# RMS norm with each row written twice: the order of loads and stores on one DMA queue, and the first loads

## The chip, the core and the metric

The kernel runs on one core of a Trainium2 chip. The time is device microseconds of one execution; 12 runs of the kernel before lie between 240.41 and 242.0 us, with a median of 241.0. A profiled execution also leaves a trace, whose span runs from the first to the last instruction. Engines are named as in the profile: ACT is ScalarE, DVE is VectorE, POOL is GpSimd, SP is SyncE; a trailing q (SPq, ACTq) is that engine's instruction queue, where transfers are issued and semaphores waited for. The transfers run on the core's 16 DMA engines.

## The reference

```python
B, S, D = 8, 512, 2048            # float32
x_rep = np.repeat(x, 2, axis=1)   # every row twice: (8, 1024, 2048)
rms = np.sqrt((x_rep ** 2).mean(axis=-1, keepdims=True) + 1e-6)
return (x_rep / rms * gamma[None, None, :]).astype(np.float32)
```

x has 4096 rows of 8 KB (33.6 MB). Each row is divided by its root mean square, multiplied by gamma, and written twice (67.1 MB).

## The kernel before

The 4096 rows are cut into 8 tiles of 512. A tile lies in SBUF as 128 partitions with K = 4 consecutive rows of x in each, so a partition's share of a load is one contiguous run of 32 KB, and its share of a store one run of 64 KB, because the repeated rows are consecutive too. One buffer `y` holds both: eight row slots in each partition, of which a load fills the upper four, and the compute writes the results to all eight. A pool of three such buffers (L39) serves the eight tiles, so tile i + 3 is loaded into the buffer of tile i, once that has been stored.

`load(i)` (L45 to L53) issues the load of tile i on SP's queue, whole (4 MB) or in `parts`. `compute` (L82) goes through a tile's four rows per partition: ACT squares a row with a running sum (L64) and takes the root (L68); DVE takes the reciprocal (L73) and multiplies the row by it and by gamma in one instruction (L74); the second copy of the row (L80) is made by ACT, for the last row of a call by DVE. ACT's square of the next row is put ahead of its copy of this one. `store(i)` (L55) issues the store of 8 MB, also on SP's queue.

The order is written by hand (`manual_schedule`, L94), and on each engine instructions go in program order. SP first issues tile 0 in four quarters (L95), then tiles 1 and 2 (L101, L102). Then, for every tile, comes its store (L108), and from tile 1 on, the load of the tile two further (L109 to L110), which has to wait until the store of the tile one before has landed, because it reuses its buffer. So the queue holds load 0, 1, 2, store 0, 1, load 3, store 2, load 4, store 3, and so on to store 7; tile 7 is loaded and stored in halves. A wait of SP for a computed tile or for a free buffer holds up all that SP issues behind it.

Gamma (8 KB) is loaded by one DMA from ACT's queue to one partition (L97); POOL broadcasts it to all 128 (L98). Every DMA from SP or ACT signals one of eight completion semaphores, which are given out in turn in the order of the program. At the end of the program (L136) SP waits for the semaphores in turn, and then all engines meet.

Of the kernel before, what the change touches and what calls it, by code (L numbers as in the profile page):

```python
# [1 line left out]

# [4 lines left out]


@with_exitstack
def kernel(  # L10
    ctx: ExitStack,
    tc: tile.TileContext,
    x: bass.AP,
    gamma: bass.AP,
    out: bass.AP,
):
    nc = tc.nc
    P = nc.NUM_PARTITIONS
    f32 = mybir.dt.float32
    Act = mybir.ActivationFunctionType  # L20
    Alu = mybir.AluOpType

    B, S, D = x.shape
    Bo, So, Do = out.shape
    R = So // S
    assert R == 2 and D == Do and B == Bo and So == S * R
    eps = 1e-6
    inv_d = 1.0 / float(D)


    K = 4
    N = B * S
    assert N % (P * K) == 0
    ntiles = N // (P * K)
    x_t = x.rearrange("b s d -> (b s) d").rearrange("(n p k) d -> n p k d", p=P, k=K)
    out_t = out.rearrange("b s d -> (b s) d").rearrange("(n p j) d -> n p (j d)", p=P, j=K * R)

    singles = ctx.enter_context(tc.tile_pool(name="singles", bufs=1))
    rows = ctx.enter_context(tc.tile_pool(name="rows", bufs=3))  # L39
    junk = ctx.enter_context(tc.tile_pool(name="junk", bufs=1, space=bass.MemoryType.PSUM))  # L40
    small = ctx.enter_context(tc.tile_pool(name="small", bufs=8))

    ys = []

    def load(i, eng, parts=1):  # L45


        y = rows.tile([P, K * R, D], f32, name="y")
        step = K // parts
        for k in range(0, K, step):  # L50
            at = K * (R - 1) + k
            eng.dma_start(out=y[:, at : at + step, :], in_=x_t[i, :, k : k + step, :])  # L52
        ys.append(y)  # L53

    def store(i, k0, k1):  # L55
        nc.sync.dma_start(  # L56
            out=out_t[i, :, R * k0 * D : R * k1 * D],
            in_=ys[i][:, R * k0 : R * k1, :].rearrange("p j d -> p (j d)"),
        )

    def square(i, k):
        sq = junk.tile([P, D], f32, name="sq")
        ss = small.tile([P, 1], f32, name="ss")
        nc.scalar.activation(  # L64
            out=sq[:], in_=ys[i][:, K * (R - 1) + k, :], func=Act.Square, accum_out=ss[:]
        )
        rms = small.tile([P, 1], f32, name="rms")
        nc.scalar.activation(out=rms[:], in_=ss[:], func=Act.Sqrt, scale=inv_d, bias=eps_t[:])  # L68
        return rms

    def scale(i, k, rms):
        rstd = small.tile([P, 1], f32, name="rstd")
        nc.vector.reciprocal(out=rstd[:], in_=rms[:])  # L73
        nc.vector.scalar_tensor_tensor(  # L74
            out=ys[i][:, R * k, :], in0=ys[i][:, K * (R - 1) + k, :], scalar=rstd[:], in1=gamma_b[:],
            op0=Alu.mult, op1=Alu.mult,
        )

    def repeat(i, k, copy):
        copy(out=ys[i][:, R * k + 1, :], in_=ys[i][:, R * k, :])  # L80

    def compute(i, k0, k1):  # L82

        rms = square(i, k0)
        for k in range(k0, k1):
            scale(i, k, rms)
            if k + 1 < k1:
                rms = square(i, k + 1)
                repeat(i, k, nc.scalar.copy)
            else:  # L90
                repeat(i, k, nc.vector.tensor_copy)


    ctx.enter_context(tc.manual_schedule())  # L94
    load(0, nc.sync, parts=K)  # L95
    gamma_b = singles.tile([P, D], f32, name="gamma_b")
    nc.scalar.dma_start(out=gamma_b[0:1, :], in_=gamma.partition_broadcast(1))  # L97
    nc.gpsimd.partition_broadcast(out_ap=gamma_b[:], in_ap=gamma_b[0:1, :])  # L98
    eps_t = singles.tile([P, 1], f32, name="eps_t")
    nc.vector.memset(eps_t, eps)  # L100
    load(1, nc.sync)  # L101
    load(2, nc.sync)  # L102

    for i in range(ntiles):
        parts = 2 if i == ntiles - 1 else 1
        for k in range(0, K, K // parts):
            compute(i, k, k + K // parts)
            store(i, k, k + K // parts)  # L108
        if i >= 1 and i + 2 < ntiles:  # L109
            load(i + 2, nc.sync, parts=2 if i + 3 == ntiles else 1)  # L110


# [1 line left out]
_INS = ['x', 'gamma']  # L114
_OUTS = [((8, 1024, 2048), 'float32')]


# [23 lines left out]
```

## Time and profile before

| | |
|---|---|
| median of 12 runs | 241.0 us (240.41 to 242.0) |
| the profiled execution | 240.41 us, span 238.6 us |
| ACT busy | 115.6 us (48%) |
| DVE busy | 90.8 us (38%) |
| queue q1 (all of x and the output), share of 16 DMA engines | 98.5% |
| moved | 100.69 MB, 422 GB/s over the span |
| load of a whole tile, median from issue to landing | 34.2 us |

The share of a queue is the time that its packets took, over 16 engines times the span. The time from issue to landing holds the time in which a transfer stands in the queue behind earlier ones; it is no measure of a transfer's own length. Idle time of an engine that isn't the bottleneck costs nothing.

### The profile page before, as it was taken

The page shows a single profiled execution, that of the slowest core. Times are in us where ns is not written, and L with a number is a line of the kernel's source. Part 1 is how long each engine was busy: PE and PEld are TensorE (multiplying, and loading weights), DVE is VectorE, ACT ScalarE, POOL GpSimd, SP SyncE. Part 2 cuts the span into 40 slices and gives each one's busy share as a digit, 9 for nine tenths or more (in the row PEclk, how much of TensorE's full clock was granted, in tenths as well). Part 3 has the DMA queues.
Part 4 walks back from the last instruction along what each step waited for, and adds up shares of the span by engine and source line. Part 5 has one row for each costly group of instructions (what it writes and reads, how often), then busy time and mean ns, then how long its engine had stood idle before and what let it go on. Part 6 is the DMA issues. An engine that isn't in the chain of part 4 may idle for free.

```text
span 238.6 us, 298 instructions
## 1 busy us (share of the span) xinstructions
DVE 90.8 (38%) x74; ACT 115.6 (48%) x121; POOL 2.5 (1%) x5
## 2 busy tenths in 40 slices
DVE  0477749671000084500864007630167219900000
ACT  2998999970000299203990049900598059600000
POOL 4000000000000000000000000000000000000000
DMA  7999998989899999999898999989998899898995
GB/s 261 430 453 439 439 439 352 527 352 527 352 434 423 450 450 397 417 428 516 352 527 352 428 450 463 417 385 439 472 461 385 385 434 522 385 494 352 434 434 220
DMA packets 3028, 100.69 MB, mean 422 GB/s; under 512 B 337, under 2 KB 337, under 8 KB 337
## 3 DMA queue, kind: packets, MB, share of 16 engines
q1 hardware_dynamic: 3024, 100.66, 98.5%
q10 hardware_dynamic: 2, 0.01, 0.0%
q14 instruction: 2, 0.02, 0.0%
HBM read 33.56 MB, written 67.11 MB: 422 GB/s over the span
## 4 chain that ended last, share of the span: by engine, by line
DMA 66%; ACT 13%; DVE 7%; SPq 1%; issue 0%
DMA y<-in_x_dram 39%; DMA out_dram<-y 27%; ACT sq L64 7%; DVE y L74 6%; ACT y L80 5%; ACT rms L68 1%; DVE y L80 1%; SPq L52 1%; DVE rstd L73 0%; SPq L56 0%
## 5 line engine op out<-in xcount | busy, mean ns | idle before, releaser
L64 ACT ACTIVATE sq<-y 128x2048 f32<-128x2048 f32 x32 | 59.9, 1872 | 85.7 <-DMA y<-in_x_dram 85.7
L74 DVE SCALAR_TENSOR_TENSOR y<-y,rstd,gamma_b 128x2048 f32<-128x2048 f32 x32 | 75.3, 2352 | 1.2
L73 DVE RECIPROCAL rstd<-rms 128x1 f32<-128x1 f32 x32 | 5.2, 162 | 116.0 <-ACT rms L68 116.0
L80 ACT COPY y<-y 128x2048 f32<-128x2048 f32 x23 | 43.4, 1888 | 3.7 <-DVE y L74 3.7
L80 DVE COPY y<-y 128x2048 f32<-128x2048 f32 x9 | 11.0, 1227 | 0.3
L68 ACT ACTIVATE rms<-ss,eps_t 128x1 f32<-128x1 f32 x32 | 9.4, 294 | 1.0
L64 ACT ACTIVATION_READ_ACCUMULATOR sq<-y 128x1 f32 x32 | 6.0, 186 | 0.0
L98 POOL PARTITION_BROADCAST gamma_b<-gamma_b x1 | 2.3, 2295 | 2.3 <-DMA gamma_b<-in_gamma_dram 2.3
L64 ACT ACT_TABLE_LOAD x1 | 1.3, 1283 | 1.3 <-PEq L125 1.3
L68 ACT ACT_TABLE_LOAD x1 | 1.3, 1283 | 0.0
L100 DVE MEMSET eps_t<- 128x1 f32 x1 | 0.1, 59 | 0.8 <-PEq L125 0.8
L125 POOL MEMSET const-bfloat16-1.0<- 128x1 bf16 x1 | 0.1, 102 | 0.0
L125 POOL MEMSET const-uint8-127<- 128x1 uint8 x1 | 0.1, 102 | 0.0
L125 POOL MEMSET const-float32-0.0<- 128x1 f32 x1 | 0.1, 99 | 0.2 <-issue 0.2
L125 POOL MEMSET const-float32-1.0<- 128x1 f32 x1 | 0.1, 100 | 0.0
## 6 DMA issues: line engine op xcount, KB each, us to landing
y<-in_x_dram SPq DMA_DIRECT2D x6, 4096.0 KB, 34.2
out_dram<-y SPq DMA_DIRECT2D x2, 4096.0 KB, 27.1
y<-in_x_dram SPq DMA_DIRECT2D x4, 1024.0 KB, 7.8
y<-in_x_dram SPq DMA_DIRECT2D x2, 2048.0 KB, 36.4
out_dram<-y SPq DMA_DIRECT2D x7, 31.7
gamma_b<-in_gamma_dram ACTq DMA_DIRECT2D x1, 8.0 KB
```

Of the source, the lines that this page charges most:

```text
L52: eng.dma_start(out=y[:, at : at + step, :], in_=x_t[i, :, k : k + step, :])
L64: nc.scalar.activation(out=sq[:], in_=ys[i][:, K * (R - 1) + k, :], func=Act.Square, accum_out=ss[:])
L68: nc.scalar.activation(out=rms[:], in_=ss[:], func=Act.Sqrt, scale=inv_d, bias=eps_t[:])
L73: nc.vector.reciprocal(out=rstd[:], in_=rms[:])
L74: nc.vector.scalar_tensor_tensor(out=ys[i][:, R * k, :], in0=ys[i][:, K * (R - 1) + k, :], scalar=rstd[:], in1=gamma_b[:], op0=Alu.mult, o ...
L80: copy(out=ys[i][:, R * k + 1, :], in_=ys[i][:, R * k, :])
L98: nc.gpsimd.partition_broadcast(out_ap=gamma_b[:], in_ap=gamma_b[0:1, :])
L100: nc.vector.memset(eps_t, eps)
L125: nc = _bacc.Bacc("TRN2", target_bir_lowering=False, num_devices=1)
```

## The change

Three things change. Tile 0 is loaded in two halves instead of four quarters. Gamma is loaded by four DMAs of 2 KB instead of one of 8 KB; the number of DMAs ahead of the stores also shifts which of the eight semaphores each later DMA signals, the last store's among them. And the loads in the loop are issued in pairs: after the stores of tiles 0 and 1 come loads 3 and 4, after the stores of 2 and 3 loads 5 and 6, after those of 4 and 5 load 7, which is in halves as before. Each load still waits for the store that frees its buffer.

```diff
-    load(0, nc.sync, parts=K)
+    load(0, nc.sync, parts=2)
     gamma_b = singles.tile([P, D], f32, name="gamma_b")
-    nc.scalar.dma_start(out=gamma_b[0:1, :], in_=gamma.partition_broadcast(1))
+    for c in range(0, D, D // 4):
+        nc.scalar.dma_start(
+            out=gamma_b[0:1, c : c + D // 4], in_=gamma[c : c + D // 4].partition_broadcast(1)
+        )
     nc.gpsimd.partition_broadcast(out_ap=gamma_b[:], in_ap=gamma_b[0:1, :])
...
             store(i, k, k + K // parts)
-        if i >= 1 and i + 2 < ntiles:
-            load(i + 2, nc.sync, parts=2 if i + 3 == ntiles else 1)
+
+        if i % 2 == 1:
+            for j in (i + 2, i + 3):
+                if j < ntiles:
+                    load(j, nc.sync, parts=2 if j + 1 == ntiles else 1)
```

## The prediction

> **What bounds the kernel now.** I read the totals and the slices first, then the queues, then the times at which SP issues each transfer, and last the start and the end.
>
> ```profile
> span 238.6 us, 298 instructions
> DVE 90.8 (38%) x74; ACT 115.6 (48%) x121; POOL 2.5 (1%) x5
> ...
> DMA  7999998989899999999898999989998899898995
> ...
> q1 hardware_dynamic: 3024, 100.66, 98.5%
> ...
> HBM read 33.56 MB, written 67.11 MB: 422 GB/s over the span
> ```
>
> No engine is busy for half of the span, while queue q1, which carries every load of x and every store, keeps the 16 DMA engines at work for 98.5% of it. The kernel is a single stream of transfers in the order in which SP issues them. It can only become faster by moving the bytes at a better rate, by losing less where one transfer gives way to the next, or at the two ends.
>
> ```profile
> 0.72 3.31 SPq L52 DMA_DIRECT2D y<-in_x_dram  x6
> 23.85 16.16 SPq L56 DMA_DIRECT2D out_dram<-y  x2
> 52.72 0.34 SPq L52 DMA_DIRECT2D y<-in_x_dram  x1
> 54.45 0.33 SPq L56 DMA_DIRECT2D out_dram<-y  x1
> 72.27 0.34 SPq L52 DMA_DIRECT2D y<-in_x_dram  x1
> 98.86 0.33 SPq L56 DMA_DIRECT2D out_dram<-y  x1
> 101.56 0.34 SPq L52 DMA_DIRECT2D y<-in_x_dram  x1
> ```
>
> This is the timeline of SP. Call the loads L0 to L7 and the stores S0 to S7 (L7 and S7 have halves a, b). L3 goes out at 52.72, when S0 has landed, L4 at 72.27 (S1 landed), L5 at 101.56 (S2 landed). By the trace's semaphore events a whole load takes 9.4 to 9.9 us (L2, just ahead of the first store, 10.7) and a whole store 19.3 to 19.7 us, one behind the other, so the queue is never dry.
>
> ```profile
> SPq L56 <- DVE y L80: 156.4, 9, 26.5
> SPq L52 <- DMA out_dram<-y: 36.6, 5, 17.5
> SPq L136 <- DMA out_dram<-y: 28.1, 3, 9.6
> ```
>
> These are SP's own waits. They are long because SP runs ahead; they cost only if a transfer is issued after the engines have run out of earlier ones.
>
> The trace also records each packet (start, bytes, duration). Undisturbed packets are very regular: 8 KB 0.309 us, 16 KB 0.61, 32 KB 1.21, 64 KB 2.418, that is 26.5 to 27.1 GB/s on each of 16 engines. What the packets took above these, summed and divided by 16, is 2.3 us: 0.54 in the first 6 us; 1.05 at 27 to 34 us, where L2 gives way to S0; 0.06, 0.11, 0.10, 0.11 and 0.10 at the five later places where a load gives way to a store; at most 0.05 in each stretch between, so a store that gives way to a load costs about nothing, nor does load after load or store after store. In each place it is the last load packets that are stretched. The 16 engines also drift apart: the spread between the first and the last one's landing is 0.6 us at S0 and 1.6 us at S7b, the end at 237.66.
>
> **The change part by part.** The sum is made against the profiled execution: 240.41 us, a span of 238.6 and 1.8 around it. It is the fastest of the 12 runs, 0.59 under their median of 241.0, so I add 0.59 at the end.
>
> *Order of the queue.* Before: L0 L1 L2 S0 S1 L3 S2 L4 S3 L5 S4 L6 S5 L7 S6 S7, six turns from load to store. After: L0 L1 L2 S0 S1 L3 L4 S2 S3 L5 L6 S4 S5 L7 S6 S7, four. Two of the five small turns go: 0.48 us / 5 x 2 = 0.19 us. Drift grows by 1.6 - 0.6 = 1.0 us over those five turns, and about half of the spread lies beyond the mean engine; two turns fewer save 1.0 x 0.5 x 2/5 = 0.2 us at the last engine, an estimate.
>
> Does the queue stay full? With 9.7 us a load, 19.4 a store and 17.0 us from a tile's landing to its store (tile 3: first square at 81.84, store issued at 98.86), the new stream runs L3 to 81.8, L4 91.5, S2 110.9, S3 130.3, L5 140.0, L6 149.7, S4 169.1, S5 188.5, L7 198.2, S6 217.6. The new wait is L4's on S1: SP issues L4 at 72.2, with L3 (9.7 us) still ahead. Behind that wait stands S2, computed by about 57; it goes out at 72.6 and is needed at 91.5. S3 can go out at 81.8 + 17.0 = 98.8, needed at 110.9. L5 waits for S2 (110.9) with S3 ahead, L6 for S3 (130.3) with L5 ahead, S4 is behind L6 on SP (130.7, needed at 149.7), S5 goes at 157.0 (needed at 169.1), S6 near 173 (198.2), S7a near 202 (217.6). Every cover is 9 us or more, so these waits cost nothing.
>
> *Tile 0 in two halves.* Per engine 32 packets of 8 KB become 16 of 16 KB: 32 x 0.309 = 9.89 against 16 x 0.611 (median of L7's packets) = 9.78 us, so 0.11 us less. SP issues two transfers fewer, 0.45 us each, hidden behind packets in flight. But the first square waits for 2 MB:
>
> ```profile
> 5.49 1.88 ACT L64 ACTIVATE sq<-y 128x2048 f32<-128x2048 f32 x1 [2.95 <-DMA y<-in_x_dram]
> ...
> 22.55 1.23 DVE L80 COPY y<-y 128x2048 f32<-128x2048 f32 x1
> ```
> ```profile
> L56 SPq EVENT_SEMAPHORE  x13: 17/6262/16983, 7.9 to 202.8; - x13
> ```
>
> The first of SP's semaphore waits on L56 marks the landing of the second quarter, 7.9. So compute of tile 0 starts 2.4 us later, and S0 goes out at 23.85 + 2.4 = 26.3. Its packets are first needed when L2's last ones end, from 30.4 on: 4 us of cover instead of 6.5. Tiles 1 and 2 follow 2.4 us later too (S1 near 42, needed at 52.6). Cost 0.
>
> On the number of transfers the trace and the Trainium skill can be weighed. The four quarters of L0 land at 5.49, 7.94, 10.43 and 12.93 us, 2.49 us apart for 1.05 MB, which is 421 GB/s, so a queued transfer pays no fixed price. The skill's page "DMA: Bandwidth & Descriptors", section "Anatomy of one DMA — SWDGE (gpsimd) path", fits a DMA as 2.0 us plus its bytes at 436 GB/s; if these queued loads paid that, two fewer would save 4 us and the sum would be 236.4. I go by the row.
>
> *Gamma in four DMAs.* One 8 KB packet becomes four of 2 KB, each with its own issue on ACT's queue and its own semaphore, and POOL's broadcast waits for all four.
>
> ```profile
> 0.71 0.51 ACTq L97 DMA_DIRECT2D gamma_b<-in_gamma_dram  x1
> ...
> 1.26 1.28 ACT L64 ACT_TABLE_LOAD   x1 [1.26 <-PEq L125]
> 2.75 2.29 POOL L98 PARTITION_BROADCAST gamma_b<-gamma_b  x1 [2.33 <-DMA gamma_b<-in_gamma_dram]
> ```
>
> Four issues end near 0.71 + 4 x 0.54 = 2.9; from the end of an issue to the broadcast it was 2.75 - 1.22 = 1.5, so the broadcast runs from 4.4 to 6.7. ACT's table load ends near 4.2. The first use of gamma is at 9.40 before, so near 11.8 after: 5 us of cover; without it every us late would delay S0, which has 4 more to give. The packets share one engine with x: gamma's packet took 0.764 us; at best four cost what one did (0), at worst 4 x 0.764 - 0.764 = 2.3 us on that engine. I take 0, since no engine stands out in the landings of the first quarter (spread 0.44 us).
>
> A rule against small transfers stands in the same page's "Rules for kernel authors": coalesce, since under 64 KB one mostly pays overhead. Its 2 us in turn for each DMA would put the broadcast at 8.7 to 11.0, an estimate from that page that would still be hidden.
>
> *The end.* S7b's semaphore moves from the sixth to the seventh of eight, and SP's closing waits go through them in turn. Behind S7b's landing the trace has two more of these, 0.06 us apart (237.68, 237.74, 237.80); one is left: 0.06 us saved.
>
> Sum: 0.19 + 0.2 + 0.11 + 0.06 = 0.56 us, 240.41 - 0.56 = 239.85, and 0.59 added for the median: **240.4 us**.
>
> **The rivals.** 0.2% of 241.0 is 0.48 us, about what a measurement of this kernel can tell from no change.
>
> *A. The turn gets dearer behind two loads (slower).* L2 to S0 costs 1.05 us and follows 29 us without a store; the small turns cost 0.10 and follow 9.7 us. If the price grows with that stretch, a turn after two loads (19.4 us) costs 0.10 + 0.95 x 9.7 / 19.3 = 0.58 by a straight line. L4 to S2 and L6 to S4 are such turns, L7 to S6 stays: 2 x 0.58 + 0.10 = 1.26 against 0.48, so 0.78 lost, 0.17 saved by the other terms, 241.0 + 0.6 = 241.6; at the full 1.05 each, 242.5. It decides from 0.28 us a turn. Against it: L2 to S0 is also the first store of all, and each of the small turns is a tenth of it.
>
> *B. Nothing reaches the end.* The engine that ends last may not be the one that lost most at the two turns; then 0.06 to 0.17 us remain, 240.9.
>
> *C. Gamma's four packets hold one engine back.* At the worst price that engine ends 2.3 us later, from a mean end of 236.4 to 238.7 against the last engine's 237.33: 1.4 us lost, less the rest, near 242.0. It decides once that engine ends later than the others.
>
> **How the numbers follow.** Forecast 0.57, A 0.20, B 0.18, C 0.05. The forecast is only just beyond the bound of 0.48; I put 0.44 of it below 240.5 and 0.13 within. B lies within but for 0.02. A and C are slower, but A with a price under 0.5 us a turn would lie within (0.03). Faster 0.46, same 0.32, slower 0.22. Low: both turns free and the whole later drift (0.5) gone, with tile 0 and the tail: 0.19 + 0.5 + 0.17 = 0.9, and 0.6 for medians that stood 0.6 above the best run: 239.5. High: A by the straight line, 241.6; beyond it lie A at the full price and C. The forecast's own range is 239.8 to 240.9.
>
> **What would show it.** Right: L3 and L4 issued near 52.6 and 72.2; S0 near 26.3; load-to-store turns of about 0.1 us near 91, 150 and 198; a smaller spread at S7b; one closing wait fewer; DMA share still above 98%. Wrong: last load packets before S2 or S4 stretched by 0.3 us or more (A), one engine alone late from the start (C), a slice under 9 tenths in the middle of the DMA row with an issue that comes after it (a dry queue, which I priced at nothing).

## The result

The changed kernel takes 240.08 us (median of 12 runs, 239.81 to 240.5), the kernel before 241.21 us (49 runs, 240.29 to 242.5). The ratio is 0.9957, with a 95% interval of 0.9943 to 0.9971: faster by 0.43%, or 1.1 us at the medians. The forecast was 240.4 us, with a range of 239.5 to 241.6. The 12 runs lie within 0.7 us, the 49 of the kernel before within 2.2. The profiled execution took 239.88 us.

### The profile after

The page of the changed kernel, totals, slices and queues:

```profile
span 238.1 us, 301 instructions
DVE 90.8 (38%) x74; ACT 115.3 (48%) x121; POOL 2.5 (1%) x5
...
DMA  7999998989899999989898999989898999998995
...
q1 hardware_dynamic: 2736, 100.66, 98.5%
...
HBM read 33.56 MB, written 67.11 MB: 423 GB/s over the span
```

The picture is the same as before: one stream of transfers, 98.5% of the DMA engines' time, and no slice under 8 tenths between the first and the last. So no wait that the change put in has let the queue run dry. The issues of SP, in order of time (start, length, and how many were merged):

```profile
0.72 1.92 SPq L52 DMA_DIRECT2D y<-in_x_dram  x4
26.51 15.13 SPq L56 DMA_DIRECT2D out_dram<-y  x2
52.56 20.03 SPq L52 DMA_DIRECT2D y<-in_x_dram  x2
72.76 26.21 SPq L56 DMA_DIRECT2D out_dram<-y  x2
110.85 19.81 SPq L52 DMA_DIRECT2D y<-in_x_dram  x2
130.77 26.43 SPq L56 DMA_DIRECT2D out_dram<-y  x2
169.41 1.32 SPq L52 DMA_DIRECT2D y<-in_x_dram  x2
171.65 37.73 SPq L56 DMA_DIRECT2D out_dram<-y  x3
```

Two loads and two stores now take turns. S0 went out at 26.51 (26.3 was worked out), L3 at 52.56 (52.6), S2 at 72.76 (72.6), L5 at 110.85 (110.9), S4 at 130.77 (130.7), L7 at 169.41 (169.1), S6 at 171.65 (near 173). SP's own waits show where the time of waiting moved:

```profile
SPq L56 <- DVE y L80: 121.2, 7, 30.2
SPq L52 <- DMA out_dram<-y: 73.3, 5, 19.3
SPq L142 <- DMA out_dram<-y: 27.7, 3, 9.6
```

SP waits twice as long for stores that free a buffer, 73.3 us instead of 36.6, and it costs nothing, because SP waits with 8 us or more of work ahead of it in the queue (L6, for one, is issued at 130.3, and the first engine ends L5 at 138.65).

Two things in the trace are shorter. The last store lands at 237.21 us instead of 237.67, and the span ends 0.89 us after that instead of 0.95. By the packet records the turns from load to store add up (excess over the undisturbed packet durations, summed and divided by 16) to 0.05, 0.17 and 0.06 us after the first one, against five that summed to 0.42 in the kernel before when measured in the same way. The spread of the engines at the end is 1.3 us instead of 1.7.

The start is where the trace differs most from what was forecast:

```profile
0.72 1.35 ACTq L98 DMA_DIRECT2D gamma_b<-in_gamma_dram  x4
...
2.10 1.28 ACT L64 ACT_TABLE_LOAD   x1 [2.10 <-issue]
8.11 1.88 ACT L64 ACTIVATE sq<-y 128x2048 f32<-128x2048 f32 x1 [4.73 <-DMA y<-in_x_dram]
8.79 2.29 POOL L101 PARTITION_BROADCAST gamma_b<-gamma_b  x1 [8.36 <-DMA gamma_b<-in_gamma_dram]
...
12.07 2.35 DVE L74 SCALAR_TENSOR_TENSOR y<-y,rstd,gamma_b 128x2048 f32<-128x2048 f32 x1 [0.15 <-DVE rstd L73]
```

ACT issued the four pieces faster than I had worked out (1.35 us), but POOL's broadcast began at 8.79, not 4.4, and ended 1 us before its first use.

### The profile page after: what moved, and what is told of

It reads as the page before. It is cut to its first block, busy times and chain, and to the rows that moved or that the text cites. A ratio compares the mean times of both kernels' runs of the same rounds, so it can differ in the third digit from the quotient of the medians.

```text
span 238.1 us, 301 instructions
## 1 busy us (share of the span) xinstructions
DVE 90.8 (38%) x74; ACT 115.3 (48%) x121; POOL 2.5 (1%) x5
## 3 DMA queue, kind: packets, MB, share of 16 engines
q1 hardware_dynamic: 2736, 100.66, 98.5%
## 4 chain that ended last, share of the span: by engine, by line
DMA 66%; ACT 14%; DVE 6%; issue 1%; SPq 0%; DVEq 0%
DMA out_dram<-y 40%; DMA y<-in_x_dram 25%; ACT sq L64 7%; ACT y L80 5%; DVE y L74 5%; ACT rms L68 1%; ACT L68 1%; DVE y L80 1%; DVE rstd L73 0%; SPq L52 0%; DVEq L74 0%; SPq L56 0%
```

## The experiments

Each is an edit of the kernel before, unless it says otherwise.

### Each part alone

The paired loads alone (`pairs_only`):

```diff
-        if i >= 1 and i + 2 < ntiles:
-            load(i + 2, nc.sync, parts=2 if i + 3 == ntiles else 1)
+        if i % 2 == 1:
+            for j in (i + 2, i + 3):
+                if j < ntiles:
+                    load(j, nc.sync, parts=2 if j + 1 == ntiles else 1)
```

> The kernel before with the loads in pairs, tile 0 in quarters and gamma in one DMA as before. If the order of the queue brings the gain (my theory: two cheap turns from load to store fewer, and less drift between the 16 DMA engines): 0.8 to 1.0 us faster than before at the median, runs as close together as those of the changed kernel (0.7 us from lowest to highest, against 2.2 us before). If the gain comes from tile 0 or from gamma: 0.0 to 0.2 us faster, and runs still spread over 2 us.

Measured: 240.31 us (239.99 to 240.6), before on the same chip 240.91 (240.18 to 242.27); ratio 0.9975, 0.9963 to 0.9988. So the order alone gains 0.6 us (0.3 to 0.9 by the interval), a little less than the 0.8 to 1.0 that I expected, and here the runs are as close together as those of the whole change (0.6 us).

Tile 0 in halves alone (`halves_only`: `parts=2` in L95):

> The kernel before with tile 0 in two halves alone. My theory: 16 KB packets in place of 8 KB ones for one tile, 0.1 us faster, spread of the runs as before (about 2 us). Rival: the start of the stream sets the drift of the engines for the rest of the run; then most of the gain of 1.0 us and the small spread show here.

Measured: 240.85 us (240.16 to 241.54), ratio 1.0000, 0.9985 to 1.0015. Neither a gain nor the small spread shows; 0.1 us is less than this interval can tell from nothing. The traces do not have it either. The engines end tile 0, in the mean, at 12.29 to 12.37 us in the seven profiles with halves, and at 12.24 to 12.33 in the seven with quarters: the packets are shorter by the 0.11 us, but the excess in the first 6 us is larger by as much (0.62 against 0.49 in the mean). At the other end something is lost: with two DMAs fewer the last store signals the fourth of the eight semaphores, and four closing waits are left behind its landing. The span ends 1.08 us after the landing, 0.13 later than before.

Gamma in four DMAs alone (`gamma4_only`):

> The kernel before with gamma in four DMAs alone. Two closing waits behind the last store's landing become another number (each 0.06 us); within 0.1 us of before by my theory, unless the first multiply now waits for gamma: with quarters it starts at 9.40 us, and the broadcast ended at 11.1 us in the changed kernel, so compute of tile 0 and store 0 come up to 1.7 us later, under 6 us of cover. Rival: which semaphore the last store uses matters for more than those waits; then 0.3 us or more faster.

Measured: 241.14 us (240.29 to 241.84), ratio 1.0002, 0.9985 to 1.002: nothing, as expected. The trace of this kernel has the wait that I had named, in small; DVE stood for 0.31 us until the broadcast was done:

```profile
7.31 2.29 POOL L101 PARTITION_BROADCAST gamma_b<-gamma_b  x1 [6.89 <-DMA gamma_b<-in_gamma_dram]
...
9.64 2.35 DVE L74 SCALAR_TENSOR_TENSOR y<-y,rstd,gamma_b 128x2048 f32<-128x2048 f32 x1 [0.31 <-POOL gamma_b L101]
```

The changed kernel with gamma in one DMA (`after_gamma1`):

> The changed kernel with gamma in one DMA again. My theory: the same time as the changed kernel within 0.1 us, that is 0.9 to 1.1 us faster than before; POOL's broadcast starts near 2.8 us instead of 8.8. Rival (gamma or the last semaphore carries part): 0.3 us or more slower than the changed kernel.

Measured: 240.32 us (239.83 to 240.77), ratio 0.9974, 0.996 to 0.9988. That is the pairs alone again. The trace has four closing waits left (span end 1.08 us after the landing, against 0.89 in the changed kernel), which is 0.19 us; the intervals of the two ratios overlap, so the medians can't confirm it.

The changed kernel once more (`after_again`):

> The changed kernel once more, for comparison on one chip with the next three: 0.9957 of before as measured first, at least 0.3 us below the pairs alone (240.31) and the changed kernel with gamma in one DMA (240.32), if the shorter row of closing waits behind the last store (one left, against two and five there, 0.06 us each) counts in unprofiled runs too.

Measured: 240.04 us (239.81 to 241.41) against 241.1, ratio 0.9961, 0.9943 to 0.9978. The first result stands, 1.1 us at the medians, but the closeness of the runs does not: they spread over 1.6 us here, as the kernel before does on this chip (1.65). The parts do not add up to the whole either. The pairs alone, the kernel with gamma in one DMA and the one below with gamma in five all stand at 0.9974 or 0.9975, about 0.6 us, and tile 0 and gamma alone at nothing; the whole change stands at 0.9957 and 0.9961, about 1.0. The intervals overlap, and the traces have no place for the other 0.4 us but 0.06 to 0.19 of closing waits (the last store lands at 237.42 in the mean of the two profiles of the changed kernel, at 237.41 in the mean of those three). It stays open. This profiled execution took 240.30 us, 0.42 more than the first profile of the same kernel; its turns cost 0.30, 0.21 and 0.03 instead of 0.05, 0.17 and 0.06, and its last store landed at 237.63 instead of 237.21. One profile is not enough to price a turn.

### More profiles of the kernel before

Two unchanged copies (`before_b`, `before_c`), for their profiles.

> The kernel before once more, for another profile of it. Runs of it lie between 240.2 and 242.5 us, and the profile shown is of one of the fastest. If the slower runs lose at the turns from load to store and by drift: a profiled execution at 241 us or more shows more excess at the five late turns than the 0.4 us (sum) of the first, and a larger spread of the engines at the end than 1.6 us, and nothing else longer. If they lose elsewhere: the same turns, and the time missing in between or ahead of the first packet.

> As for the other copy of the kernel before; two looks, since about half of its runs are above 241 us.

They took 241.24 and 240.47 us. The second is a twin of the first profile. The first is one of the long runs:

```profile
span 239.5 us, 298 instructions
...
q1 hardware_dynamic: 3024, 100.66, 98.2%
```

The packets of q1 took 98.2% of the engines' time here and 98.5% in the first profile: nothing waits for SP, some engines simply finish early. By the 4-byte packets with which each engine ends a transfer, the engines end (us, first to last) as follows; in brackets the excess at the turn:

```
turn        before (240.41)             before_b (241.24)           after (239.88)
L2 to S0    32.41..33.03                32.48..33.11                32.32..32.85
L3 to S2    80.73..81.47   (0.04)       80.88..81.89   (0.28)       -
L4 to S3    109.78..110.67 (0.10)       109.91..111.24 (0.05)       -
L4 to S2    -                           -                           90.32..91.01   (0.05)
L5 to S4    138.80..139.97 (0.09)       139.14..140.94 (0.29)       -
L6 to S5    167.94..169.12 (0.10)       168.14..169.94 (0.02)       -
L6 to S4    -                           -                           148.47..149.60 (0.17)
L7 to S6    196.98..198.64 (0.09)       197.18..199.49 (0.15)       196.89..198.20 (0.06)
end of S7   235.66..237.32              235.86..238.17              235.57..236.88
```

The spread changes mainly at these rows. Between them (a load after a store, a store after a store) it changes by at most 0.11 us (in S2 of `before_b`), so what an engine loses at a turn it mostly keeps to the end. The long run lost 0.79 us in the mean at its five turns instead of 0.42, and its last engine ended 0.85 us later than in the first profile. Over five profiles of the old order (three of the kernel before, gamma and halves alone) the last store lands at 237.30 to 238.51, mean 237.87; over five of the new order (the changed kernel twice, pairs alone, gamma in one and in five DMAs) at 237.17 to 237.66, mean 237.42. From the end of L2 to the end of S7b the engines take 203.68 us in the mean of the five old ones (203.53 to 203.94) and 203.49 in that of the five new ones (203.38 to 203.64), and the last engine stands 1.09 and 0.90 us behind the mean one.

### The price of a turn

More turns with the same transfers. Tiles 1 to 6 are stored and tiles 3 to 7 loaded in halves, and the halves take turns (`split_more_turns`; `only` picks a half of a load) or not (`split_same_turns`):

```diff
         compute(i, 0, K)
         store(i, 0, 2)
-        store(i, 2, 4)
-        if i + 2 < ntiles:
-            load(i + 2, nc.sync, parts=2)
+        if i + 2 < ntiles:
+            load(i + 2, nc.sync, parts=2, only=0)
+        store(i, 2, 4)
+        if i + 2 < ntiles:
+            load(i + 2, nc.sync, parts=2, only=2)
```

(minus: same turns, plus: more turns; the new argument of `load` is not shown)

> The kernel before with tiles 1 to 6 stored in halves and tiles 3 to 7 loaded in halves, one half of each in turn: ten late turns from load to store instead of five. By my theory, 0.1 us a turn in the mean and about as much again by drift: 0.5 to 1.0 us slower than the kernel with the same halves in the old order, and a larger spread between the engines at the end. Rival (turns cost nothing, the pairs gain by something else): the same within 0.2 us.

> The control for the kernel with more turns: the same halves, but both halves of a store and then both halves of a load, so five late turns as before. By both theories what the smaller packets cost against before, at 27.0 instead of 27.1 GB/s per engine for the stores: 6 stores, 8 packets of 64 KB at 2.418 us against 16 of 32 KB at 1.213 each, 0.06 us a store, so 0.4 us slower than before.

Measured: 242.95 us (241.86 to 243.24, 6 runs) with ten late turns, ratio to before 1.0068, 1.0045 to 1.0092; 241.37 us (240.82 to 242.45) with five, ratio 1.002, 1.0002 to 1.0038. First the page of the kernel with more turns, then that of its control:

```profile
span 241.3 us, 321 instructions
...
DMA  7999998989999999999999999999999999999993
...
q1 hardware_dynamic: 4464, 100.67, 98.2%
```
```profile
span 239.6 us, 324 instructions
...
DMA  7999998989999999999999999999999999999994
...
q1 hardware_dynamic: 4464, 100.67, 98.5%
```

The same packets and bytes, no dry stretch in either, and 1.6 us more span. The 16 engines end 237.03 to 240.10 and 236.20 to 238.46: in the mean 0.92 us later, the last one 1.64 later. Five turns more cost 242.95 - 241.37 = 1.58 us at the medians, 0.32 us each (0.23 by the two ratios): a bit over half (0.92 / 5 = 0.18) is lost by every engine in the mean, the rest is drift. This is well above the 0.5 to 1.0 that I expected, and it answers the rival that turns cost nothing. The control itself stands 0.3 us above the kernel before at the medians, where 0.4 was expected. Two turns fewer at 0.23 to 0.32 are 0.46 to 0.63 us, and the pairs alone gained 0.60.

Three stores, then three loads, on the changed kernel (`triples`):

```diff
-        if i % 2 == 1:
-            for j in (i + 2, i + 3):
-                if j < ntiles:
-                    load(j, nc.sync, parts=2 if j + 1 == ntiles else 1)
+        for j in {2: (3, 4, 5), 4: (6, 7)}.get(i, ()):
+            load(j, nc.sync, parts=2 if j + 1 == ntiles else 1)
```

> The changed kernel with three stores, then three loads: S0 S1 S2 L3 L4 L5 S3 S4 L6 L7 S5 S6 S7. The turn from L5 to S3 comes after 29 us without a store, as long as before the first store. Rival A of the prediction (a turn's price grows with the stretch without a store): the last packets of L5 are stretched by 0.8 to 1.0 us, and the run is 0.6 us slower than the changed kernel. If the first turn is dear because it holds the first store of all: about 0.1 us at that turn, and with two late turns instead of three the run is 0.1 to 0.3 us faster than the changed kernel. S3 is issued only some 2 us ahead of its need here; a turn at 0.8 us or more with S3 late would leave the two causes mixed, which its issue time will tell.

Measured: 240.86 us (239.83 to 242.08), ratio to before 0.998, 0.9958 to 1.0002; so there is no gain over the changed kernel (240.04 on the same chip) but a median 0.8 us higher, with one turn fewer; the intervals overlap. The runs spread over 2.2 us. SP's issues, and the queue's share:

```profile
118.16 15.13 SPq L56 DMA_DIRECT2D out_dram<-y  x2
140.52 19.95 SPq L52 DMA_DIRECT2D y<-in_x_dram  x3
160.59 0.37 SPq L56 DMA_DIRECT2D out_dram<-y  x1
```
```profile
q1 hardware_dynamic: 2736, 100.66, 98.7%
```

S3 went out at 118.16, before the first engine was done with L5 (119.34). The turn from L5 to S3, after 29 us without a store, cost 0.00 us. The turn from L7 to S5, after 19 us, cost 0.82, though S5 had been issued 18 us ahead. And the last packets of S4, a store behind a store, were stretched by 0.24 us in the mean, ahead of L6. So the stretch without a store is not by itself what makes a turn dear (rival A's rule falls), and neither does only the first store pay such a price. What makes one turn cost 0.8 us or more and another nothing is open; that S3 was issued barely ahead of its need may be a part of it, which no run separates. The share of the queue does not show such a loss: a stretched packet counts as busy, and 98.7% is the highest share of these pages.

### The dear first turn, and one more DMA

The changed kernel, but a first quarter of store 0 goes out from ACT's queue, while SP's queue still streams L1 and L2 (`early_write`; that `store` also takes the queue as an argument is not shown):

```diff
+        if i == 0:
+            compute(0, 0, 2)
+            store(0, 0, 1, nc.scalar)
+            compute(0, 2, 4)
+            store(0, 1, 4)
+            continue
```

> The changed kernel, but the first row pair of store 0 (2 MB) goes out from ACT's queue at about 16.5 us, while SP's queue still streams L1 and L2. It is after the 1.0 us at the turn from L2 to S0. If that is the price of the first store of all: the early store pays it beside the loads, the turn from L2 to S0 falls to about 0.1, and the run is 0.5 to 0.9 us faster than the changed kernel. If a turn can cost up to 1 us at any place, as the turn from L7 to S5 did with three loads in a row: no gain (within 0.3 us), the two queues' packets alternate and the price appears there or at the old place.

Measured: 239.72 us (239.36 to 240.29, 11 runs), before on the same chip 240.55; ratio 0.9971, 0.9959 to 0.9984. The early store was issued at 16.65:

```profile
16.65 0.38 ACTq L56 DMA_DIRECT2D out_dram<-y  x1
```

The turn from L2 to S0 is then smooth (no packet there is stretched by over 0.08 us), and q1's packets that start at 18 to 22 us are stretched by 0.72 us in the mean, 0.43 of it ahead of the early store's first packet (21.01). So most of the first turn's price (0.88 and 1.15 us in the two profiles of the changed kernel) has moved to where the first store now meets the loads. In the mean the engines end at 235.87 us, against 236.05 and 236.46 in those two. It is the lowest median of all, but the kernel before was faster in these runs too: 0.83 us are gained on it, not the 1.1 of the changed kernel. Whether it beats the changed kernel is not settled.

The changed kernel with gamma in five DMAs (`gamma5`: four pieces, the last one cut in two):

> The changed kernel with gamma in five DMAs, so that the last store signals the last of the eight semaphores and no closing wait is left behind it: 0.06 us faster than the changed kernel in the profile's last microsecond, which the median of 12 runs will hardly tell (within 0.15 us of 240.04). Against it: gamma's fifth piece lands some 0.7 us later, the broadcast ends near 11.8 us, and the first multiply, ready at 11.92, waits by at most 0.3 us, under some 4 us of cover for store 0.

Measured: 240.23 us (239.45 to 240.65), ratio 0.9974, 0.9959 to 0.9988. The span ends 0.83 us after the last landing, 0.06 less than in the changed kernel, and DVE waited 0.37 us for the broadcast. The median does not tell it from the changed kernel.

## Why the prediction held, and where it was off

**The queue stays full: right.** The issue times worked out from 9.7 us a load, 19.4 a store and 17.0 a tile's compute were met within 0.3 us, but for S6's, which came 1.4 us sooner. SP's longer waits cost nothing.

**Two turns fewer: right, and in size as well as the runs can tell.** The step gave 0.19 for the turns and 0.2 for the drift, 0.39 in all. Five profiles of each order give 203.68 - 203.49 = 0.19 in the mean and 1.09 - 0.90 = 0.19 at the last engine, though the five of one order scatter by more than that. The pairs alone gained 0.60, with 0.39 inside the interval (0.3 to 0.9), and the pair of kernels in halves would give 0.46 to 0.63. That the sizes came out of a single profile and held is partly luck: its late turns summed to 0.42, those of the long run to 0.79, and `triples` shows that counting turns alone does not carry far.

**The 0.59 us added for the median: wrong.** The working took the distance between the profiled execution and the median for a constant. The median of the changed kernel lies 0.20 above its first profile and, in `after_again`, 0.26 below the profile: the distance says only where in the spread of the runs the profiled execution fell. With 0.20 in place of 0.59 the sum would have given 240.05, against 240.08. For the profile itself the sum gave 239.85 us against 239.88 measured, and that closeness is luck too: `after_again` took 240.30, and in the first profile tile 0 ended 0.08 us later instead of 0.11 earlier, while the first turn happened to cost 0.88 instead of 1.04.

**Tile 0 in halves: wrong by the 0.11 us.** The packets are shorter as worked out, but the first ones of the run are stretched more, and tile 0 is done no earlier. No fixed price per queued transfer showed: two loads fewer left the ratio at 1.0000, so the 4 us did not appear that the fit on the skill's page "DMA: Bandwidth & Descriptors", section "Anatomy of one DMA — SWDGE (gpsimd) path", would have given; these loads go out from SP's queue.

**Gamma in four: cost right (0), working wrong.** The step that failed is "from the end of an issue to the broadcast it was 1.5". It holds for the first piece alone, whose packet ran at 1.62 to 2.11 us. The packets of the others started at 5.55, 6.85 and 7.55, each with its 4-byte semaphore packet some 0.7 us behind. The skill's page "DMA: Bandwidth & Descriptors", section "Queues, rings and completion order", says that a DMA engine takes its queues in turn, a packet from each. That agrees with the 0.7 us between the later packets, one 16 KB packet of x (0.61) and the small one, if each packet record of the trace counts as a packet; the page gives 9 to 17 descriptors as typical for one. It does not explain the 3.4 us from 2.11 to 5.55, which stays open. Of the 5 us of cover, 0.84 was left (broadcast done at 11.08, first use ready at 11.92). The estimate of 8.7 to 11.0 that the prediction made from the page came out at 8.79 to 11.08, but not for its reason: the four landed at 2.1, 6.2, 7.5 and 8.2 us and not 2 us apart.

**The closing waits: right.** 0.95 to 0.89 us. With four, two, one and none of them left the traces show 1.08, 0.95 (0.93 in `gamma4_only`), 0.89 and 0.83 us.

**The rivals.** A, at 0.28 us a turn or more: the turns behind two loads cost 0.02 to 0.30 us over five profiles, above 0.28 only once in ten. Their mean is 0.14, against 0.10 for the late turns of the old order: a little dearer, but far from the 0.58 of A's straight line, and its rule fell with `triples`. B: the gain did reach the end. C: gamma's packets held nothing up that shows; the engines ended L2 within 0.53 us of each other, closer than before (0.62).

## What to carry to other kernels

Where one queue keeps the DMA engines busy to 98%, its share does not tell what is lost inside. Look at where it turns from loads to stores, and at how far apart the engines are at the end: with the same packets, five turns more cost 0.23 to 0.32 us each here, over half of it in every engine and the rest by drift. Loads in pairs gained; with three in a row, one turn fewer still, nothing more was gained, so try a grouping and do not count turns alone. Take the price of a turn from several profiles, and do not carry the distance between a profile and the median over to another kernel.

## What the runs showed of the hardware that I had not expected

- The price of a turn from load to store is not fixed: 0.02 to 0.30 us (mean over the engines) at the late turns of the ten profiles in the old and the paired order, 0.00 and 0.82 in `triples`, and 0.88 to 1.19 at the first turn of those ten. Other places, behind the first 6 us, cost at most 0.05 us in the ten; S4 in `triples` cost 0.24.
- The engines' drift is mostly kept. Of the spread between the first and the last one, 0.3 to 0.7 us was there by the end of L1; it was 0.5 to 0.8 us after the first turn and 1.2 to 2.3 at the end (in whole tiles; 3.1 with ten late turns). Behind the first turn it grew at turns from load to store and in a store directly behind one (there by up to 0.23 us), and changed elsewhere by at most 0.05, but for `triples`, where late packets of S4 narrowed it by 0.35.
- Transfers on ACT's queue, beside a full queue from SP, started late: of four 2 KB pieces issued by 2.07 us the last ended at 8.24 us, and the 2 MB that `early_write` issued there at 16.65 had their first packet at 21.01.
